# Sixteen kilobytes moved from the DMA scratch to a tile arena: two more expert-weight slots in each layer of a hybrid diffusion trunk

## The chip, the cores and the metric

The kernel runs on one core of one Trainium2 chip, in fp32 (matmul operands are fp32, or fp32r pairs of a high and a low part). The metric is the device time of one execution in microseconds; the time of a kernel is the median of its runs.

## What is computed

Two trunk layers over 256 latent tokens and 256 context tokens of width 1024. Each layer modulates and normalizes its tokens, projects them, runs four mixers (retention, window attention, neighbourhood attention, gated delta rule), merges these with sigmoid gates, projects out, and then runs a mixture of experts. Layer 0 carries all 512 tokens on; layer 1 only the 256 latent ones.

```
mod  = silu(c) @ w_mod + b_mod                       # six rows of 1024, for latent and context
h    = rmsnorm(x, norm1) * (1 + sc1) + sh1
z    = h @ w_in                                      # 1024 x 5904
ys   = retention(z), window(z), neighbourhood(z), gdn(z)
acc  = sum_i sigmoid(h @ w_merge[i]) * (ys[i] @ w_branch[i])
x    = x + g1 * (acc @ w_out)
h2   = rmsnorm(x, norm2) * (1 + sc2) + sh2
e    = top-2 experts of the best of 8 groups of 4    # 32 experts, routed by a sigmoid
x    = x + g2 * sum_e w_e * (silu(h2 @ w_e_gate[e]) * (h2 @ w_e_up[e])) @ w_e_down[e]
```

The experts' weights are 3 x 2 MB for each of the 32 experts, so each layer reads 192 loads of 1 MB.

## The kernel before

**Memory.** Nearly all tiles live in two arenas that the kernel manages itself: `arenaF` (fp32, `FKB` = 136 KB per partition, in segments `FSEG`, the last one 64 KB) and `arenaR` (fp32r, 56 KB). `Arena.alloc` takes a zone (an address range) and, unless `first` is set, the place in it that was given back longest ago. Python decides all addresses ahead of time; the framework then orders each engine's instructions by their place in the program and by estimated times, and adds the waits for tiles that are still in use. The zones are constants at the top of the file: `ZRAW` (0 to 16 KB, raw weights on their way to being split), `ZPRJ` (103 KB to the end, rings of the dense section), `ZMIX[l]` (merge, residual and expert scratch) and `ZW[l]` (the expert weights' slots). `ZW[0]` and `ZW[1]` start at 16 KB; `ZMIX[l]` starts where `ZW[l]` ends.

**The dense part of a layer** (`dense`, L1492). Projections, mixers and gates run interleaved, with weights loaded by SP into `ZRAW` (L242) and split in two by ACT and DVE or GpSimd. The gates' tanh goes to DRAM (`th`, L1356) and comes back in `merge` (L1391), where it multiplies the branch products `pbr`. The section's rings are allocated from the low end of `ZPRJ` and given back when the section ends (L1540), ahead of `merge`. By their sizes in the code they take 23 KB: five work buffers of 2 KB, `zt` 4, `prow` 3.25, `rt` 2, `jk`, `rtab` and `abw` 1 each, `ptmp` 0.5, `ab` 0.25.

**Modulation rows.** `mod` (L318) computes 2048 columns of the modulation at a time. The first call stands at the kernel's start; five more calls (40 loads of 1 MB of w_mod, 160 matmuls into `pmod`) are a filler in layer 0, of which one step is taken at a time, at places in the retention and attention part (`fill`, L346). Their zone is `ZPRJ`: a bias row `sb` of 2 KB from the low end, and for each load a buffer of 8 KB:

```python
for k in range(2):
    w = self.F.alloc((128, 4, 512), *zone)
    nc.sync.dma_start(w, wm[:, 2 * kk + k, c0:c0 + 2048].rearrange("p (j n) -> p j n", j=4))
    for j in range(4):
        nc.tensor.matmul(ps[32 * j:32 * j + 32], self.sc[:, 2 * kk + k, :], w[:, j], ...)
    self.F.free(w)
```

**Experts** (`moe`, L1898). After out-projection and routing, `wslots` (L1770) makes the slots for expert weights, 8 KB per partition (1 MB) each:

```python
slots = [(self.F, o) for o in range(ZW[l][0], ZW[l][1] - n + 1, n)]
slots.sort(key=lambda v: self.F.since(v[1], n))
...
late = 3 if l else 0
self.wq += reg[:len(reg) - late] + once + reg[len(reg) - late:]
```

`ZW` holds 9 slots in layer 0 and 11 in layer 1; layer 1 adds two of `arenaR`; and in both layers three places (two of `arenaR`, one of `ZRAW`) serve once. So 12 loads can be under way before the first matmul in layer 0, and 16 in layer 1. Slots that were given back earlier are used first. The out-projection's buffers (`ZTR`) lie on some of them, and in layer 0 the neighbourhood mixer's output `yk` lies at 95 to 103 KB until its turn, the last, in `merge`.

Experts run in pairs (`mlp`, L1822): gate (4 loads, 32 matmuls), up (4), down (4). SP issues the loads in the order gate of pair 0, up 0, gate 1, down 0, up 1, gate 2, down 1 and so on (L1800), each into the slot at the head of a queue; a slot goes back to its end after its matmuls. All loads and stores of the kernel are issued by SP, in one order.

Of the kernel before, what the change touches and what calls it, by code (L numbers as in the profile page):

```python
# [22 lines left out]
OFF = {'ret_q': 0, 'ret_k': 256, 'ret_v': 512, 'ret_g': 1024, 'win_q': 1536, 'win_k': 2048, 'win_v': 2176,  # L23
       'na_q': 2304, 'na_k': 2816, 'na_v': 3328, 'gdn_q': 3840, 'gdn_k': 4352, 'gdn_v': 4864, 'gdn_g': 5376,
       'gdn_ab': 5888}
FKB, RKB, WLO = 136, 56, 32
FSEG = (16, 16, 16, 16, 8, 64)
RSEG = (16, 16, 8, 8, 8)
KB = lambda a, b: (a * 256, b * 256)

# [4 lines left out]
      ((2, 1, 2, 1), (1, 1, 1, 1, 1, 1), (2, 1, 2, 1), (2, 2, 1, 2)))  # L35
FD = ((0, 10, 2), (6, 28, 4))
FT = 1, 3
ZW = (KB(16, 88), KB(16, 106))
ZMIX = (KB(88, FKB), KB(106, FKB))
ZYK = (KB(95, 103), KB(106, FKB))  # L40
ZATT = ((KB(16, 32), KB(72, 103)),)
ZTR = (KB(56, 88), KB(74, 98))
ZRET = (KB(48, 64), KB(72, 103)),
# [90 lines left out]
class Net:  # L134
    def __init__(self, tc, ctx, a, dbg):
# [6 lines left out]
        self.sp = p("sp", 1)  # L142
        self.F = Arena(self.big, [k * 256 for k in FSEG], F32, "arenaF")
        self.R = Arena(self.big, [k * 256 for k in RSEG], F32R, "arenaR")
# [1347 lines left out]
    def dense(self, l):  # L1492
# [25 lines left out]
        self.zone = ZATT  # L1518
        self.yk = self.F.alloc((128, 4, nt), *ZYK[l])
        self.done = {}  # L1520
# [20 lines left out]
        self.aside = False  # L1541
        self.zone = ZMIX[l]
        with self.use(1):
# [226 lines left out]
    def wslots(self, l):  # L1770
# [4 lines left out]
        self.wq = deque()  # L1775
        slots = [(self.F, o) for o in range(ZW[l][0], ZW[l][1] - n + 1, n)]
        slots.sort(key=lambda v: self.F.since(v[1], n))
# [287 lines left out]
```

## Time and profile before

| | |
|---|---|
| median of 3 runs | 2553.84 us (2551.1 to 2556.44) |
| profiled execution: its own time | 2552.03 us |
| its span, first to last instruction | 2550.3 us |
| PE busy (matmul) | 2341.4 us, 92% |
| DVE, ACT, GpSimd busy | 52%, 32%, 20% |
| bytes read from HBM, written to HBM | 609.85 MB, 30.16 MB |
| mean granted clock of TensorE | 0.970 |

The two expert stages lie at about 996 to 1470 us (layer 0) and 2085 us to the end (layer 1). Busy shares are averages over stages with different limits.

### The profile page before, as it was taken

What the parts mean: (1) busy time and instruction counts of PE and PEld (TensorE: products, weight loads), DVE (VectorE), ACT (ScalarE), POOL (GpSimd) and SP (SyncE); (2) the same over time, 40 slices, a digit from 0 to 9 for tenths busy, and PEclk for the clock granted to TensorE, in tenths of its full rate; (3) what the DMA queues carried; (4) which work ended last, traced back from release to release, by engine and by line L of the source; (5) the groups of instructions that cost most, each with busy time, mean ns of one, the idle gap of its engine ahead of it and who ended that gap; (6) DMA issues with size and microseconds to landing.
All of it is one profiled execution on the core that took longest, in us unless ns stands there. A gap on an engine that the chain in (4) does not pass through costs nothing. (4 is left out here: it accounts for less than half of the span.)

```text
span 2550.3 us, 38070 instructions
## 1 busy us (share of the span) xinstructions
PE 2341.4 (92%) x14396; PEld 1596.1 (63%) x14396; DVE 1321.4 (52%) x3284; ACT 818.2 (32%) x1810; POOL 518.0 (20%) x491
## 2 busy tenths in 40 slices
PE   6989899999999987999999989998899879999897
PEld 3777787676666884444545478998788854433332
DVE  5674754275456676333333268795777652222222
ACT  3443343244455342110101155444467321101100
POOL 2222313241210540111111221010411410000001
PEclk8999999999999998999999989999899989999999
DMA  7235425655556655999999934735236869999997
GB/s 273 83 106 159 108 84 174 201 187 205 208 186 230 222 166 191 401 420 419 420 419 419 385 91 114 210 109 149 92 102 216 266 233 420 419 420 419 420 419 315
DMA packets 269196, 642.56 MB, mean 252 GB/s; under 512 B 64336, under 2 KB 194768, under 8 KB 213072
## 3 DMA queue, kind: packets, MB, share of 16 engines
q1 hardware_dynamic: 269008, 640.07, 68.1%
q8 instruction: 115, 1.88, 0.3%
q14 instruction: 73, 0.60, 0.1%
HBM read 609.85 MB, written 30.16 MB: 251 GB/s over the span
## 5 line engine op out<-in xcount | busy, mean ns | idle before, releaser
L177 POOL TENSOR_TENSOR arenaF<-arenaF 128x512 f32<-128x512 f32 (+3 forms) x226 | 252.3, 1129 | 1217.1 <-DVE arenaF L177 933.5
L281 PE MATMUL pd<-arenaR,arenaR 128*128 128x256 f32 (+1 forms) x1152 | 359.9, 313 | 8.1 <-ACT arenaR L423 3.2
L282 PE MATMUL pd<-arenaR,arenaR 128*128 128x256 f32 (+1 forms) x1152 | 354.5, 308 | 12.4 <-DVE arenaR L177 12.1
L283 PE MATMUL pd<-arenaR,arenaR 128*128 128x256 f32 (+1 forms) x1152 | 351.9, 306 | 0.0
L177 DVE TENSOR_TENSOR arenaR<-arenaF,arenaR 128x512 fp32r<-128x512 f32 (+2 forms) x366 | 283.2, 788 | 116.6 <-ACT arenaR L249 81.8
L249 ACT ACTIVATE arenaR<-arenaF 128x512 fp32r<-128x512 f32 (+1 forms) x348 | 247.7, 721 | 207.2 <-PE pbr L282 58.6
L165 PE MATMUL pw_e_up<-arenaF,arenaF 128*64 128x512 f32 x952 | 233.6, 595 | 25.6 <-DMA arenaF<-in_w_e_up_dram 25.6
L281 PEld LDWEIGHTS pd<-arenaR,arenaR 128*128 128x128 f32 x1152 | 225.3, 196 | 27.3 <-issue 9.6
L282 PEld LDWEIGHTS pd<-arenaR,arenaR 128*128 128x128 f32 x1152 | 225.4, 196 | 23.5 <-DVE arenaR L177 15.5
L283 PEld LDWEIGHTS pd<-arenaR,arenaR 128*128 128x128 f32 x1152 | 225.3, 196 | 9.1 <-issue 2.8
L165 PE MATMUL pw_e_gate<-arenaF,arenaF 128*64 128x512 f32 x920 | 219.1, 598 | 0.0
L177 DVE TENSOR_TENSOR arenaR<-py,arenaR 128x512 fp32r<-128x512 f32 x64 | 44.3, 692 | 319.1 <-ACT arenaR L1875 318.1
L165 PE MATMUL py<-arenaF,arenaF 128*64 128x512 f32 x672 | 193.0, 594 | 3.3 <-DMA arenaF<-in_w_e_down_dram 2.4
L165 PEld LDWEIGHTS pw_e_up<-arenaF,arenaF 128*64 128x64 f32 x952 | 79.0, 137 | 164.4 <-issue 112.3
L281 PE MATMUL pgate<-arenaR,arenaR 128*128 128x512 f32 (+1 forms) x512 | 178.5, 349 | 3.0 <-ACT arenaF L688 2.1
L283 PE MATMUL pgate<-arenaR,arenaR 128*128 128x512 f32 (+1 forms) x512 | 178.1, 348 | 2.6 <-DVE arenaR L177 2.6
L282 PE MATMUL pgate<-arenaR,arenaR 128*128 128x512 f32 (+1 forms) x512 | 176.4, 345 | 0.0
L177 POOL TENSOR_TENSOR arenaR<-arenaF,arenaR 128x1024 fp32r<-128x1024 f32 (+1 forms) x48 | 111.1, 2316 | 229.3 <-ACT arenaR L249 207.3
L177 DVE TENSOR_TENSOR arenaF<-arenaF 128x128 f32<-128x128 f32 (+30 forms) x368 | 132.8, 368 | 8.0 <-ACT arenaF L864 1.8
L186 DVE SCALAR_TENSOR_TENSOR arenaF<-pw_e_up,ws,arenaF 128x512 f32<-128x512 f32 x32 | 24.0, 751 | 213.8 <-PE pw_e_up L165 213.8
L1860 ACT ACTIVATE arenaF<-pat 128x512 f32<-128x512 f32 x32 | 19.1, 597 | 360.1 <-PE pat L1858 360.1
L165 PEld LDWEIGHTS pw_e_gate<-arenaF,arenaF 128*64 128x64 f32 x920 | 63.5, 136 | 110.7 <-issue 103.2
(400 smaller groups left out, 4384.4 us busy)
## 6 DMA issues: line engine op xcount, KB each, us to landing
arenaF<-in_w_e_up_dram SPq DMA_DIRECT2D x119, 1024.0 KB, 12.1
arenaF<-in_w_e_down_dram SPq DMA_DIRECT2D x117, 1024.0 KB, 16.1
arenaF<-in_w_e_gate_dram SPq DMA_DIRECT2D x116, 1024.0 KB, 12.8
arenaF<-in_w_mod_dram SPq DMA_DIRECT2D x48, 1024.0 KB, 5.3
arenaF<-in_w_in_dram SPq DMA_DIRECT2D x92, 512.0 KB, 4.1
arenaF<-in_w_merge_dram SPq DMA_DIRECT2D x64, 512.0 KB, 4.0
arenaF<-in_w_branch_dram SPq DMA_DIRECT2D x32, 512.0 KB, 4.8
arenaF<-in_w_out_dram SPq DMA_DIRECT2D x24, 512.0 KB, 4.4
```

Of the source, the lines that this page charges most:

```text
L165: self.tc.keep_in_program_order(self.nc.tensor.matmul(out, lhs, rhs, start=start, stop=stop))
L177: (eng or self.nc.vector).tensor_tensor(out=out, in0=a, in1=b, op=op)
L186: self.nc.vector.scalar_tensor_tensor(out, a, s, b, op0=op0, op1=op1, accum_out=accum)
L249: self.nc.scalar.activation(h, src, AF.Copy)
L281: mm(ps, L[0], R[0], start=first, stop=False)
L282: mm(ps, L[0], R[1], start=False, stop=False)
L283: return mm(ps, L[1], R[0], start=False, stop=last)
L1860: nc.scalar.activation(aT[:, :, :np_], pt[:, :, :np_], AF.Copy)
```

## The change

The scratch that the program reserves in SBUF for dynamic DMAs goes from 16 KB (the default) to 2 KB per partition. `arenaF` grows by 16 KB: its last segment from 64 to 80 KB. The expert slots' zones `ZW` grow by 16 KB, so they hold 11 slots in layer 0 and 13 in layer 1. `ZMIX`, and `ZYK` in layer 1, move up by 16 KB at the same size. `ZDENSE` (16 KB to the end) and `ZPRJ` (103 KB to the end) are written with `FKB` and so grow by 16 KB.

```diff
-FKB, RKB, WLO = 136, 56, 32
-FSEG = (16, 16, 16, 16, 8, 64)
+FKB, RKB, WLO = 152, 56, 32
+FSEG = (16, 16, 16, 16, 8, 80)
...
-ZW = (KB(16, 88), KB(16, 106))
-ZMIX = (KB(88, FKB), KB(106, FKB))
-ZYK = (KB(95, 103), KB(106, FKB))
+ZW = (KB(16, 104), KB(16, 122))
+ZMIX = (KB(104, FKB), KB(122, FKB))
+ZYK = (KB(95, 103), KB(122, FKB))
...
-    nc = _bacc.Bacc("TRN2", target_bir_lowering=False, num_devices=1)
+    nc = _bacc.Bacc("TRN2", target_bir_lowering=False, num_devices=1, dynamic_dma_scratch_size=2048)
```

## Rows read from the trace of the kernel before

**Rows 1.** The page's 40 slices of the span: GB/s moved by DMA.
```profile
GB/s 273 83 106 159 108 84 174 201 187 205 208 186 230 222 166 191 401 420 419 420 419 419 385 91 114 210 109 149 92 102 216 266 233 420 419 420 419 420 419 315
```

**Rows 2.** Busy time by stretch: its length, PE, PEld, DVE, ACT, POOL, clock, DMA.
```profile
core 0: us, PE busy (x) PEld busy (x) DVE busy (x) ACT busy (x) POOL busy (x), PEclk, DMA share, GB/s
400.00:760.00 360.00, 339.61 (x2111) 243.34 (x2111) 180.50 (x500) 148.50 (x352) 93.28 (x87) 0.99 0.58 198
...
996.00:1460.00 464.00, 462.12 (x2292) 217.73 (x2290) 164.59 (x317) 47.92 (x80) 73.31 (x56) 1.00 1.00 409
...
1960.00:2060.00 100.00, 92.27 (x748) 86.58 (x746) 58.45 (x118) 45.77 (x97) 34.72 (x36) 1.00 0.78 256
...
2072.00:2080.00 8.00, 1.69 (x7) 1.51 (x7) 6.65 (x34) 0.00 (x0) 0.00 (x0) 0.50 0.63 267
2080.00:2089.00 9.00, 8.93 (x43) 5.86 (x43) 5.93 (x33) 2.03 (x5) 0.00 (x0) 0.76 0.00 0
...
2200.00:2500.00 300.00, 272.43 (x1248) 110.66 (x1248) 76.07 (x153) 29.86 (x50) 25.93 (x21) 1.00 1.01 420
```

**Rows 3.** The chain that ended last: start us, length us, what.
```profile
1977.40 5.25 DMA arenaF<-th
...
2504.18 19.89 DMA arenaF<-in_w_e_up_dram
2524.11 3.66 PE pw_e_up L165 x14
```

**Rows 4.** SP's issues in layer 1: start, duration of the group, line, how many.
```profile
1887.30 0.34 SPq L1800 DMA_DIRECT2D arenaF<-in_w_e_gate_dram  x1
...
2069.80 0.33 SPq L1800 DMA_DIRECT2D arenaF<-in_w_e_down_dram  x1
2088.76 6.50 SPq L1800 DMA_DIRECT2D arenaF<-in_w_e_up_dram  x4
...
2506.68 7.80 SPq L1800 DMA_DIRECT2D arenaF<-in_w_e_down_dram  x4
```

**Rows 5.** PE's waits, 996 to 1470 us: total, times, longest.
```profile
PE pw_e_up L165 <- DMA arenaF<-in_w_e_up_dram: 0.3, 1, 0.3
```

**Rows 6.** SP's issues in layer 0's expert stage, two rounds.
```profile
1058.37 6.77 SPq L1800 DMA_DIRECT2D arenaF<-in_w_e_down_dram  x4
...
1087.98 6.77 SPq L1800 DMA_DIRECT2D arenaF<-in_w_e_down_dram  x4
```

**Rows 7.** PE in order of time, layer 0's expert stage: an early and a late group.
```profile
1028.31 7.04 PE L165 MATMUL pw_e_up<-arenaF,arenaF 128*64 128x512 f32 x32
...
1415.85 7.52 PE L165 MATMUL pw_e_up<-arenaF,arenaF 128*64 128x512 f32 x32
```

**Rows 8.** DMA queues, whole span: packets, MB, share of 16 engines.
```profile
q1 hardware_dynamic: 269008, 640.07, 68.1%
```

**Rows 9.** SP's issues of w_mod in layer 0's attention part.
```profile
481.64 0.33 SPq L331 DMA_DIRECT2D arenaF<-in_w_mod_dram  x1
...
489.64 0.33 SPq L331 DMA_DIRECT2D arenaF<-in_w_mod_dram  x1
...
741.31 0.33 SPq L331 DMA_DIRECT2D arenaF<-in_w_mod_dram  x1
```

**Rows 10.** The page's DMA issues: count, size, median us to landing.
```profile
arenaF<-in_w_mod_dram SPq DMA_DIRECT2D x48, 1024.0 KB, 5.3
...
arenaF<-th SPq DMA_DIRECT2D x32, 256.0 KB, 3.5
```

**Rows 11.** SP's waits, 400 to 760 us.
```profile
SPq L331 <- DMA arenaF<-in_w_mod_dram: 55.5, 15, 7.0
...
SPq L331 <- PE pmod L333: 42.5, 22, 7.8
```

**Rows 12.** PE's waits, 400 to 760 us.
```profile
PE pmod L333 <- DMA arenaF<-in_w_mod_dram: 9.5, 9, 2.1
```

**Rows 13.** SP's issues in layer 0's merge.
```profile
800.32 0.69 SPq L1800 DMA_DIRECT2D arenaF<-in_w_e_gate_dram  x1
```

**Rows 14.** PE's waits, 796 to 832 us.
```profile
PE pbr L281 <- DVE arenaF L186: 3.8, 1, 3.8
```

## Prediction

> **What bounds the kernel now.** I read the slices of the page first, for the places where DMA is full: two plateaus of about 420 GB/s, the expert stages of the two layers, and before each of them a long stretch of mostly 80 to 270 GB/s [rows 1]. Then the stretches by stage, to see for each plateau whether PE is full beside DMA [rows 2]. In layer 0 (996 to 1460 us) PE is busy 462.12 of 464 us: it has no time left, so PE sets the end there. In layer 1 (2200 to 2500) PE is busy 272.43 of 300 us and the DMA share is 1.01: DMA sets the end there. The chain of waits says the same: its late part is one weight load of 19.9 us after another, up to the last matmuls [rows 3].
>
> In layer 1 a load of 1 MB costs 1.0486 MB / 420 GB/s = 2.50 us of a full DMA [rows 2]; the 19.89 us of a link of the chain are then 8 loads in flight. The plateau starts when SP gets the first slot back, at 2088.76 [rows 4]. Until then the 16 slots have taken 16 of the layer's 192 loads, from 1887.30 to 2069.80; between 2080 and 2089 DMA moves nothing at all [rows 2]. From 2088.76 on, 176 loads are left: 176 x 2.50 = 440 us, which gives 2528. The last four were issued from 2506.68 to about 2514 [rows 4], so the last landed some 20 us later, at 2534. "First free slot plus what is left" is 6 us short in 445; as a law of differences it should hold better: each load taken before 2088.76 ends the kernel 2.50 us earlier.
>
> **The change part by part.**
>
> *Two more slots in layer 1.* They cover 104 to 120 KB, where the rings of the dense section were, which are given back before the merge (its `th` loads are on the chain from 1977 [rows 3]). They are sorted ahead of the slots under the out-projection's buffers, so two loads of the second pair's gate weights go into them early, and the two slots of arenaR take the first two up loads of the second pair, which before waited for 2088.76. DMA has room for them: a share of 0.78 over 1960 to 2060, 0.63 in 2072 to 2080, nothing in the 9 us after [rows 2]. They need 5 us. Bounds: 0 if they are issued only after 2088, and -5.0 us if both land before. I take -5.0: DMA is full from there to the end, so nothing swallows it. The cover is PE's slack: 300 - 272 = 28 us in the 300 shown, far more than 5, so PE doesn't become the bound.
>
> *Two more slots in layer 0.* PE waits for a weight only once between 996 and 1460, 0.3 us [rows 5], and SP comes round every 29.61 us per pair of experts, 1058.37 to 1087.98 [rows 6], where 12 loads need 12 x 2.50 = 30.0. So DMA loses 0.4 us a pair and the stock of filled slots runs dry only at the very end: a late group of up matmuls takes 7.52 us where an early one takes 7.04 [rows 7]. Bounds: 0, and three times that stretch, 1.5 us, if the two groups of weights after it are as late. I take -1.
>
> *The scratch.* The program's transfers, 640.07 MB, went through one queue of the kind hardware_dynamic [rows 8], and every issue in the profile is SP's. The trace doesn't show the scratch. I cost it at nothing; what it would cost if loads in flight needed it stands with the rivals.
> The Trainium skill (DMA: Bandwidth & Descriptors, section SWDGE vs HWDGE vs iDMA) says that only transfers whose descriptors GpSimd writes keep rings in SBUF, and that those issued from SP never touch that path; by it this part is exactly 0. No run here shows it so far.
>
> *A side effect on layer 0's modulation loads, which the change doesn't name.* The zone ZPRJ grows from 33 to 49 KB with the arena. The dense section's rings take its first 23 KB (see above) and the bias row of `mod` 2 KB, so 8 KB were left: exactly one buffer for the 40 loads of w_mod that are strewn through the attention part. The trace has this: successive loads of w_mod are 8 us apart (481.64 and 489.64), the last goes out at 741.31 [rows 9], though one lands in 5.3 us [rows 10], and SP stands still before such an issue for 55.5 + 42.5 us [rows 11] with other loads behind it. PE pays 9.5 us in 9 waits for w_mod [rows 12]. With 16 KB more there are three buffers, so a load can go out two loads (16 us) ahead of its use, against 5.3 us of landing. In 400 to 760 PE is busy 339.61 of 360 us [rows 2], so this stage is PE's too, and its 20 us of gaps are all there is to win. Bounds: -9.5 if each of the nine waits goes and nothing takes its place; 0 if other gaps open (the order of instructions is made anew from estimates, and matmuls of `mod` that now come early no longer fill later gaps). I take the middle, -5: nine waits of about 1 us in a stream that is 94% busy should partly reappear.
>
> *What the early loads collide with.* In both layers the added loads may go out during the merge, whose `th` loads are short and urgent: the one at 1977.40 holds the chain for 5.25 us [rows 3]. In layer 0 the two new slots overlap the buffer `yk` (95 to 103 KB), so they come free in the last quarter of the merge. The like has happened before: an expert load went out at 800.32 among the merge's loads [rows 13], and PE lost 3.8 us on a branch product around there [rows 14]. Four more such loads: from 0 to 4 x 3.8 = 15 us. PE is busy 92.27 of 100 us in layer 1's merge [rows 2] with most of its early expert loads out, so most of them cost nothing visible. I take +2, half a collision.
>
> Sum: -5.0 - 1 - 5 + 2 = -9 us. Against the profiled execution's 2552.03 (span 2550.3 and 1.7 around it) that gives 2543; the median of the three runs is 1.8 above that execution, so for a median I say 2545. A measurement of this kernel tells about 0.2%, 5.1 us, from no change.
>
> **Rivals.**
>
> *Layer 1 alone.* The modulation loads pay nothing, because PE's gaps only move: -5.0 - 1 + 1.5 = -4.5, 2549. For it: 20 - 9.5 = 11 us of PE's gaps in that stage have other causes, so other work runs late there too. Against it: SP's 98 us behind w_mod. 0.24, half of it inside 0.2%.
>
> *Everything pays.* -5.0 - 1.5 - 9.5 and no collision: -16, 2538. 0.10.
>
> *The slots come too late.* SP issues in one fixed order; if the added loads are put behind an issue that waits for the routing, they reach DMA only around 2088 and the change doesn't do what it says: nothing in layer 1, and with other gaps opening at w_mod about 0 in all, 2553. Against it: SP issued nothing from 2070 to 2088 [rows 4], since it had no slot to fill. 0.08.
>
> *Slower: prefetch ahead of the `th` loads.* Place: the merges. One queue serves both; a `th` load behind two weight loads comes 2 x 2.50 = 5.0 us later than its 3.5 us [rows 10], and DVE, then PE, wait. Each collision costs 3.8 us [rows 14]. With nothing won at w_mod, two of them (7.6) eat the 6 us of the expert stages, so it decides from two on; all four give 15 - 6 = +9, 2563. 0.10.
> The Trainium skill (DMA: Bandwidth & Descriptors, section Queues, rings and completion order) says that each DMA engine takes the descriptors of one issuer's ring in order, so a late `th` can't overtake a weight load; by it a collision costs what is queued ahead. The trace agrees in one place, with the 3.8 us.
>
> *The scratch bounds the loads in flight.* One load at a time would take the 5.3 us that a load of this size takes by itself [rows 10] in place of 2.50: 384 x 2.8 = 1075 us more. Nothing in the trace speaks for it; under 0.01.
>
> **How the numbers follow.** Forecast 0.48, layer 1 alone 0.24, everything 0.10, too late 0.08, slower 0.10. Faster by over 0.2%: 0.44 of the forecast's 0.48, 0.11 of layer 1 alone, and 0.10: 0.65. Within 0.2%: 0.04 + 0.13 + 0.08 = 0.25. Slower: 0.10. The likeliest gives 2545, with its own range 2540 to 2549. The range for 8 in 10 runs from just past "everything" to 2 us past "too late": 2537 to 2555. It leaves out the slower case and a tail of the best one.
>
> **What would show it.** Right: in layer 1 eighteen expert loads issued before the first slot comes back, and 5 us less between the first gate matmul and the end; in layer 0's expert stage a length within 1.5 us of before; in the attention part w_mod loads issued in groups, PE's waits for them near 0, and the last of them well before 741. Wrong: a longer merge, with PE or DVE waiting for `th`; the same number of early loads as before; new PE gaps in the attention part of the size of those that went.

## The result, and the profile after

The changed kernel takes 2515.01 us (median of 4, 2513.18 to 2521.81) where the kernel beside it takes 2554.89: a ratio of 0.9851, 95% interval 0.9831 to 0.9871. It is faster by about 40 us, more than four times the 9 us of the forecast and outside its range. Timed twice more, each time beside the kernel before on the same chip, it gave 0.9848 and 0.9835.

The page of the kernel after: busy times, and the DMA's slices, which answer to [rows 1].

```profile
PE 2312.6 (92%) x14396; PEld 1586.1 (63%) x14396; DVE 1333.0 (53%) x3284; ACT 815.6 (32%) x1810; POOL 519.2 (21%) x491
...
GB/s 283 112 108 162 110 85 170 221 201 265 206 154 246 222 141 248 400 419 419 420 419 419 324 105 132 199 109 145 93 119 223 269 250 419 420 419 419 420 419 320
```

PE is busy 92% of the span, as before, but 28.8 us less: the same 14396 records take less time. (A record is one row of the trace; an fp32 product of `py` or `pmod` leaves two.) So most of the gain lies in what the profile calls busy, not in PE's waits. To find where, here are the windows of both kernels by the same four stages: layer 0's attention part from the first filler product to the first branch product, layer 0's merge, layer 0's expert stage and layer 1's. Before:

```profile
411.50:784.50 373.00, 354.24 (x2189) 252.42 (x2189) 197.60 (x557) 165.17 (x397) 96.60 (x94) 0.99 0.59 201
...
784.50:908.10 123.60, 117.11 (x576) 93.08 (x575) 78.97 (x147) 47.10 (x96) 40.44 (x28) 0.97 0.68 223
995.80:1476.30 480.50, 474.05 (x2337) 225.07 (x2336) 177.09 (x334) 50.99 (x85) 81.03 (x64) 1.00 0.97 397
2085.20:2550.30 465.10, 424.69 (x1968) 172.00 (x1968) 121.50 (x258) 48.89 (x82) 38.60 (x30) 0.99 0.97 400
```

After:

```profile
409.30:763.00 353.70, 335.34 (x2188) 252.59 (x2188) 206.09 (x564) 164.41 (x400) 97.78 (x94) 0.98 0.62 211
...
763.00:879.80 116.80, 114.79 (x575) 90.48 (x574) 78.91 (x140) 45.88 (x94) 41.04 (x28) 1.00 0.72 241
969.50:1446.20 476.70, 469.74 (x2337) 218.62 (x2336) 176.83 (x333) 51.30 (x86) 81.35 (x65) 1.00 0.96 396
2052.40:2511.40 459.00, 422.85 (x1969) 173.37 (x1968) 121.83 (x260) 49.04 (x82) 38.53 (x30) 1.00 0.97 401
```

The attention part is 19.3 us shorter, the merge 6.8, the expert stages 3.8 and 6.1: 36.0 of the span's 38.9 us. The other stretches differ by 6 us at most, in both directions. The expert stages and the merge repeat well: over all the profiles layer 1's expert stage takes 458.9 to 460.8 us with the two new slots and 463.8 to 465.2 without, and layer 0's merge 123.2 to 125.2 us where its zone stays and 116.7 to 118.8 where it moves (but for the two runs further down whose new order shifts that boundary). In the attention part PE does the same products in 18.9 us less of busy time; its idle time is about the same (18.8 and 18.4 us), and its clock is not higher.

SP's issues after, which answer to [rows 9] and [rows 4] (start, duration of the group, line, how many):

```profile
434.54 2.41 SPq L331 DMA_DIRECT2D arenaF<-in_w_mod_dram  x2
459.93 2.42 SPq L331 DMA_DIRECT2D arenaF<-in_w_mod_dram  x2
490.79 0.88 SPq L331 DMA_DIRECT2D arenaF<-in_w_mod_dram  x2
...
650.48 0.33 SPq L331 DMA_DIRECT2D arenaF<-in_w_mod_dram  x1
...
1855.69 0.34 SPq L1800 DMA_DIRECT2D arenaF<-in_w_e_gate_dram  x1
...
2037.15 0.33 SPq L1800 DMA_DIRECT2D arenaF<-in_w_e_down_dram  x1
2056.11 0.80 SPq L1800 DMA_DIRECT2D arenaF<-in_w_e_up_dram  x2
```

The loads of w_mod now go out in groups of up to three, the last 91 us earlier than in [rows 9]. From 1855.69 to 2037.15 there are 18 expert loads before the first slot comes back at 2056.11; in [rows 4] there were 16. PE's waits after, 400 to 740 us, which answer to [rows 12], and behind them a wait of before (400 to 760 us) that [rows 12] doesn't show:

```profile
PE ppt L1330 <- DVE arenaF L186: 7.2, 3, 3.7
PE ppt L1330 <- DVE arenaF L177: 3.4, 1, 3.4
...
PE pmod L333 <- issue: 0.8, 1, 0.8
```

```profile
PE ppt L1330 <- DVE arenaF L186: 2.5, 2, 2.2
```

No wait for a w_mod load is left, but the transposes `ppt` now wait 10.6 us for the softmax on DVE, where they waited 2.7 before.

### The profile page after: what moved, and what is told of

Same layout as the page of the kernel before. It is cut to its first block, busy times and chain, and to the rows that moved or that the text cites. A ratio compares the mean times of both kernels' runs of the same rounds, so it can differ in the third digit from the quotient of the medians.

```text
span 2511.4 us, 38022 instructions
## 1 busy us (share of the span) xinstructions
PE 2312.6 (92%) x14396; PEld 1586.1 (63%) x14396; DVE 1333.0 (53%) x3284; ACT 815.6 (32%) x1810; POOL 519.2 (21%) x491
## 5 line engine op out<-in xcount | busy, mean ns | idle before, releaser
L165 PE MATMUL pw_e_up<-arenaF,arenaF 128*64 128x512 f32 x952 | 225.2, 594 | 20.0 <-DMA arenaF<-in_w_e_up_dram 20.0
L165 PE MATMUL py<-arenaF,arenaF 128*64 128x512 f32 x608 | 176.0, 593 | 2.8 <-DMA arenaF<-in_w_e_down_dram 1.9
L165 PEld LDWEIGHTS pw_e_up<-arenaF,arenaF 128*64 128x64 f32 x952 | 71.8, 137 | 160.0 <-issue 123.1
```

The costliest lines, as they stand in the source:

```text
L165: self.tc.keep_in_program_order(self.nc.tensor.matmul(out, lhs, rhs, start=start, stop=stop))
```

## The parts of the change, each by itself

**The scratch.** This is the kernel before, with `dynamic_dma_scratch_size=2048` and nothing else.

> Before with the scratch of 2 KB alone; no zone changes. Both theories: within 0.2% of before (5 us), the same order of instructions on every engine. If the scratch itself or the shift of addresses that it brings were worth something, it would show here.

Measured: 0.9996 (0.9978 to 1.0013). The smaller scratch costs and brings nothing that can be told from 0.2%. That fits what the Trainium skill (DMA: Bandwidth & Descriptors, section SWDGE vs HWDGE vs iDMA) says of transfers that SP issues.

**The modulation loads.** Slots and zones as before; only the filler's zone gets the new 16 KB. In the second run it gets 8 of them.

```diff
-ZDENSE, ZIN, ZPRJ, ZRAW = KB(16, FKB), KB(16, 48), KB(103, FKB), KB(0, 16)
+ZDENSE, ZIN, ZPRJ, ZRAW = KB(16, 136), KB(16, 48), KB(103, 136), KB(0, 16)
...
-            self.filler = itertools.chain(*(self.mod(*q) for q in ((0, 1, ZPRJ), ...
+            self.filler = itertools.chain(*(self.mod(*q) for q in ((0, 1, KB(103, 152)), ...   # second run: 144
```

> Only the filler's zone for w_mod grows (three buffers instead of one); expert slots, the merge's zones and everything else stay where they were before. Theory 'order': with the modulation loads no longer late, PE's order around them is made with fewer changes between kinds of matmul, and the same matmuls run closer together; so the stretch from the first filler load to the first branch product falls from 370.7 to about 352 us, PE's busy time in it from 352 to about 333, and the kernel by 19 to 27 us (19 of that stretch, up to 7 of the merge behind it, whose first yr buffer waits for the last w_mod). Rival 'waits only': what was lost were PE's nine waits of 9.5 us; the kernel falls by at most 10 and PE's busy time stays at 352. Rival 'slots and room': the gain hangs on the slots and the larger merge zone; within 4 us of before.

> As the run with three buffers, but the filler's zone is 8 KB larger instead of 16: two buffers for w_mod. A load can then go out one load, about 8 us, ahead of its use, against 5.3 us of landing. Theory 'order': it comes on time, so nearly the whole gain of three buffers, 15 to 25 us. Rival 'the gain grows with the distance': half of what three buffers give, about 10 us. Rival 'slots and room': within 4 us of before.

Measured: 0.9916 (0.9892 to 0.9940) with three buffers, 21.8 us by the medians; 0.9928 (0.9905 to 0.9951) with two, 17.4 us. So this side effect is over half of the whole gain, and two buffers can't be told from three. The attention part with three buffers, to be read against the 373.00 of before:

```profile
413.30:768.60 355.30, 336.30 (x2189) 252.31 (x2188) 204.59 (x563) 163.24 (x397) 97.80 (x94) 0.98 0.61 206
```

It is 17.7 us shorter, with 17.9 less of PE busy time: nearly what the whole change does there. Merge and expert stages stay within 1 us of before, so the gain in the merge that was expected of this run didn't come.

**Slots and merge.** The first run is the change with the filler held to 33 KB; the second has only the slots, put into the new 16 KB; the third moves only layer 0's merge zone.

```diff
+((0, 1, KB(103, 136)), ...                           # all three: one buffer for w_mod
...
+        slots += [(self.F, o * 256) for o in (136, 144)]      # slots only; ZW, ZMIX as before
...
-ZMIX = (KB(88, 136), KB(106, 136))
+ZMIX = (KB(104, FKB), KB(106, 136))                           # room only; ZW as before
```

> The change as it is, but the filler keeps its 33 KB, so one buffer for w_mod as before. Theory 'order': the stretch from the first filler load to the first branch product stays at 371 us (within 3) with PE busy 352 in it; what is left is the merge and the expert stages, 10 to 17 us in all, of which layer 1's expert stage 5 to 6. Rival 'slots and room': 30 to 40 us, as the whole change.

> Only two more expert slots in each layer, in the new 16 KB (136 to 152 KB); one buffer for w_mod and the merge's zones as before. Theory: layer 1's expert stage 5 us shorter (two loads more before the first slot comes back), layer 0's 4 to 5 us (its up matmuls stay at 6.97 us a group instead of stretching to 8.3 from the ninth group on), merge of layer 0 within 2 us of before; 8 to 11 us in all. Rival 'a hidden cost of prefetch in the merge': less than 6.

> Only layer 0's merge zone moves, from 88-136 KB (of which 8 KB are taken by yk until its last quarter) to 104-152 KB (48 KB free at once); slots and w_mod's one buffer as before. Theory 'room': the stretch from the first branch product to the first router product falls from 123.6 to about 118 us, nothing else moves: 4 to 7 us. Rival 'the merge gains through the slots' or 'through the earlier end of w_mod': within 2 us of before.

Measured: together 0.9942 (0.9924 to 0.9961), 15.2 us; slots alone 0.9963 (0.9951 to 0.9976), 9.6 us; room alone 0.9992 (0.9980 to 1.0005), 3 us by the medians, which can't be told from no change, though its merge is shorter. The product of three buffers and of slots with merge is 0.9916 x 0.9942 = 0.9858, the whole change 0.9851: the parts add up.

Slots alone: layer 1's expert stage goes from 465.10 to 460.00 us and layer 0's from 485.30 to 480.80, each here up to the next norm's first transpose, which is some 5 us later than in the windows above. The merge, with the early loads beside it, takes 124.40 and layer 1's 110.5 (123.60 and 110.3 before), so these loads cost at most 1 us there. First layer 0's stage before, then both stages of the slots-only run:

```profile
995.80:1481.10 485.30, 474.07 (x2338) 225.09 (x2337) 180.10 (x345) 53.88 (x92) 82.28 (x66) 1.00 0.96 395
```

```profile
1005.70:1486.50 480.80, 469.86 (x2337) 219.37 (x2336) 179.97 (x345) 53.86 (x92) 82.20 (x66) 0.99 0.97 399
2091.80:2551.80 460.00, 422.90 (x1969) 172.71 (x1968) 121.46 (x258) 48.96 (x82) 38.55 (x30) 1.00 0.97 400
```

Room alone: the merge's window, and PE's waits there, 760 to 912 us:

```profile
796.30:914.40 118.10, 116.30 (x574) 92.06 (x573) 78.74 (x147) 46.52 (x95) 40.66 (x28) 0.99 0.70 226
```

```profile
PE pbw L1436 <- DVE bwc L1433: 0.9, 1, 0.9
PE pout L281 <- ACT arenaR L1407: 0.9, 1, 0.9
```

The merge is 5.5 us shorter and the 3.8 us wait of [rows 14] is gone, though the early expert loads still go out beside it. What ended that wait is in SP's rows. Before, the first pair of `th` loads is issued 21 us after the merge's start at 784.50, and SP waits ahead of it for the attention product `py`, 4.8 us at the longest; a `th` load can depend on `py` only through the place that it goes to. In the room-only run the pair goes out 4 us after the merge's start at 796.30. First two rows of before (SP's waits, 784 to 832 us, and its issues), then the issue in the room-only run:

```profile
SPq L1391 <- PE py L1337: 5.2, 2, 4.8
...
805.82 1.19 SPq L1391 DMA_DIRECT2D arenaF<-th  x2
```

```profile
800.15 0.81 SPq L1391 DMA_DIRECT2D arenaF<-th  x2
```

So the wait was not the queue behind an expert load: the merge had no place for `th`. Its zone of before begins at 88 KB, among the addresses up to 103 KB that attention and `yk` use. In the run with slots and merge this wait is gone too, and by the medians that run gains 5.6 us more than the slots alone (on two chips). That the room-only kernel shows less in its time is not explained: the profiled execution, the slowest of its 12, had an attention part of 382.1 us, and the same part, in the order of before and with one buffer, took 373.0, 371.8, 374.1 and 379.0 us in the profiles of before, of the small scratch, of slots with merge and of slots alone. It differs by 10 us from one profile to the next, so a difference of a few us there means little in a single profile.

## Why the attention part got shorter: order or lateness

With three buffers PE's order changes between the 2057th and the 4041st of the 11494 matmul instructions that can be pinned as shown below, and nowhere else. Two things therefore came together: loads that are on time, and a new order. An order can be pinned without any wait, by edges between neighbours that hold only for issue (shortened here):

```python
pe = [i for i in nc.cur_bb.bb.instructions if i.engine == mybir.EngineType.PE and ...]
for a, b in zip(order, order[1:]):
    tc.add_manual_dep(pe[b], pe[a].name, mybir.DependencyInfo(mybir.DependencyClass.NoSync, ...), reason="pin")
```

One run has three buffers with the order of before, the other one buffer with the order that three buffers give.

> The kernel with three buffers for w_mod, but all PE matmuls pinned (issue order only, no added waits) to exactly the order that they have in the kernel before; so the loads can come early and PE's order is the old one. Theory 'order and lateness both': with gaps sorted by the pair of matmul kinds on either side, the three-buffer run lost 10.6 of its 17.7 us by a different mix of neighbours and 7.2 by shorter waits; so here the stretch from the first filler load to the first branch product falls by about 7 (to 366), and the kernel by 7 to 10 us. Rival 'order alone': within 3 us of before. Rival 'lateness alone': the whole 18 us of the stretch, 22 of the kernel, whatever the order.

> The kernel before with its one buffer for w_mod, but all PE matmuls pinned to exactly the order that they have in the kernel with three buffers. Rival 'order alone': the whole gain, 15 to 22 us. Theory 'order and lateness both': this order runs the matmuls of two loads back to back, and with one buffer the second load can only be issued when the first one's matmuls are over; each of the 20 pairs then makes PE wait for a load that takes 5.3 us or more, so 60 to 130 us slower than before.

Measured: early loads in the old order 0.9966 (0.9952 to 0.9980), 9.3 us; and once more:

> Three buffers with PE's old order once more, on the chip of the other three: 0.9966 of before, within 0.002, by every theory; what the old order with products rejoined is compared with.

0.9952 (0.9934 to 0.9971), 13.4 us. The new order with late loads: 1.0494 (1.0469 to 1.0520), 126 us slower; PE then waits for w_mod:

```profile
PE pmod L333 <- DMA arenaF<-in_w_mod_dram: 112.3, 23, 7.8
```

So early loads by themselves are worth 9 to 13 us, about the 9.5 that [rows 12] gave as a bound; the new order adds the other 8 to 13 of the 21.8 (a difference of runs on different chips), and it pays only with the buffers. The attention part of the two old-order runs:

```profile
413.00:776.20 363.20, 353.80 (x2188) 251.35 (x2188) 197.71 (x557) 165.28 (x397) 96.61 (x94) 0.99 0.62 200
```

```profile
408.40:773.30 364.90, 355.44 (x2190) 252.69 (x2189) 198.20 (x558) 165.14 (x397) 96.66 (x94) 0.98 0.59 199
```

Against the 373.00 of before, early loads in the old order leave PE's busy time where it was (354 us) and halve its idle time, 18.8 to 9.4 us: that is the waits for w_mod. The new order then takes 18 us off the busy time and gives 10 us of idle time back (336 of 355 us). So a PE that was 97% busy ran an order in which the same products cost more.

**What in the order?** Call products that write the same tile one kind. Counted from the trace's records of this part, neighbours are of different kinds 332 times in the old order and 256 times in the new, and 297 and 326 records start within 0.01 us of the one before. The first suspect was the change of kind. Two runs pin the changed kernel's order with runs of projection and gate products put together.

> The changed kernel with PE's order pinned to its own, but for the attention part of layer 0, where each run of at most six projection or gate matmuls that is followed by at most 16 others is put behind these, to the next run of its kind: 232 runs of one kind in place of 284. Theory 'changes of kind cost PE time': early loads with the new order had 76 changes fewer than early loads with the old order and the stretch was 7.9 us shorter, about 0.10 us a change (an estimate from those two runs); 52 fewer are worth about 5 us, so 5 us less than the changed kernel run beside it and PE's busy time in the stretch 5 us lower. Rival 'the mix of neighbours is worth nothing by itself': within 2 us of the changed kernel, busy time the same. Rival 'delay costs more': the matmuls put off are waited for, 3 us or more slower than the changed kernel.

> As the run with longer runs in the attention part, and also in the delta-rule part before it (runs of at most three, put behind at most twelve others: 294 runs in place of 339). Theory: 45 changes fewer there, about 4.5 us more, so some 9 to 10 us less than the changed kernel. Rival: PE waits there for DVE and ACT anyway, and what is put off is late: 0, or a loss of some us in the first 411 us.

Measured: 0.9863 (0.9842 to 0.9883) and 0.9878 (0.9859 to 0.9897), beside the changed kernel:

> The changed kernel again, beside the others on the same chip. Every theory: 0.985 of the kernel before, within 0.002; it is what the two kernels with longer runs are compared with.

0.9848 (0.9824 to 0.9873). So neither is faster, and the second is more likely slower (2525.5 against 2519.5 us): the theory fails as stated. The part's own window can't be compared, since its end has moved in the new order. From the first filler product to the first router product the first of these runs took 477.1 us with PE busy 450.6, the changed kernel 472.3 with 451.9: busy time fell by 1 us where 5 were expected, and idle time rose by 6. PE gets new waits, of the transposes for ACT, which empties their PSUM tile:

```profile
PE ppt L1330 <- ACT arenaF L1331: 3.9, 5, 2.0
```

The changed kernel has no such row. That the products put off had been covering this is likely but not shown. Fewer changes alone don't pay.

The second suspect was products that lie in different halves of the array (`py` writes 64 of 128 PSUM partitions with each) and start side by side when they are neighbours. One run rejoins 29 such groups in the old order, one parts those of `py` in the changed kernel's order with the kinds left as they are, by the order of its loops:

```diff
-        for j in range(nj):
-            for e in range(2):
+        for e in range(2):
+            for j in range(nj):
```

> Three buffers and PE's old order, as in the run with early loads and old order, but 29 groups of products that the old order parts are put side by side again (12 pairs of py, 15 of psc, 2 groups of pmod); changes of kind 346 instead of 356, so nearly as many. Theory 'parted products': counted over four kernels, the stretch without its waits moves by 0.30 to 0.37 us for each pair of records that start together, so these 29 give back 6 to 9 us of the 7.9 that the old order costs: near the run with three buffers, 0.993 or less of before. Rival 'changes of kind': ten fewer, 1 us; as the old order. Rival 'neither': within 2 us of the old order.

> The changed kernel with the same sequence of kinds on PE, but inside each py tile the four products of one column half come first and then those of the other, so that no two neighbours lie in different halves. Theory 'parted products': 16 records of py, which took 1.88 us, take about 16 x 0.21 = 3.4; for the 320 records of the kernel 20 to 30 us slower than the changed kernel, 12 to 18 of them in the stretch. Rivals: changes of kind are the same, so within 2 us of the changed kernel.

Measured: parted 0.9892 (0.9869 to 0.9915), 8 to 13 us slower by the medians than the changed kernel (2527.5 against 2519.5 and 2514.7, timed apart from it), where 20 to 30 were expected. The rows of a `py` group of 16 and of one of 8 (start, duration), first in the changed kernel timed again, then parted:

```profile
579.39 1.95 PE L1337 MATMUL py<-arenaF,arenaF 128*64 128x256 f32 x16
...
613.14 1.08 PE L1337 MATMUL py<-arenaF,arenaF 128*64 128x256 f32 x8
```

```profile
579.02 2.86 PE L1337 MATMUL py<-arenaF,arenaF 128*64 128x256 f32 x16
...
614.57 1.09 PE L1337 MATMUL py<-arenaF,arenaF 128*64 128x256 f32 x8
```

Parting costs 0.91 us in a group of 16; six of them in this part make 5.5 us, and the part was 5.7 longer (360.2 against 354.5). The mechanism is real but weaker than expected: a group of 16 takes 2.86 us parted and not 3.4, and a group of 8 loses nothing, since its products still start in pairs 0.01 us apart. Rejoined in the old order: 0.9948 (0.9930 to 0.9966), no different from the old order's 0.9952. Its attention part:

```profile
413.00:775.30 362.30, 348.98 (x2189) 248.01 (x2189) 198.03 (x565) 164.61 (x397) 97.05 (x94) 0.99 0.60 202
```

PE is busy 4.8 and 6.5 us less than in the two runs of the old order, but the part is only 0.9 and 2.6 us shorter: the rest went into idle time. Only 16 more pairs of records came to start together, none of them of `py`, so this run tests half of what it set out to. It shows at most 2.6 of the 8 to 10 us that the order is worth in this part as the price of parted products. The remainder has no single cause that a run here showed; cheaper products and newly opened waits came together in every order that was tried.

**The same cure without memory, and a better order.** One run has half-size loads in the 8 KB of the kernel before; two rejoin in the changed kernel the products that its own order parts.

> The kernel before, with no memory moved, but each load of w_mod split into two of half the size (two of the four column blocks each), so that the 8 KB of one buffer hold two. Theory 'lateness and order': the next half can come while the last one is multiplied; the stretch falls by a part of what two full buffers gave (16 of 18 us), 4 to 10 us, if the four column blocks still run side by side. Rival 'blocks apart': the four 32-column products of one load no longer start together, and each load costs up to 0.5 us more, 20 us in 40 loads: slower than before by 5 to 20 us.

> The changed kernel with the 11 groups rejoined that its own order still parts in that stretch (3 pairs of py, 4 of psc, 4 groups of pmod). Theory 'parted products': 2 to 4 us less than the changed kernel (0.9848 to 0.9851 of before), so about 0.9837. Rivals: no difference.

> The changed kernel with the 11 parted groups of layer 0 rejoined, and the 3 of layer 1 too. Theory 'parted products': the run that parted 58 pairs of records on purpose lost 5.6 us in the stretch, 0.1 us a pair, and the rejoined run's stretch was 3.0 us shorter than the changed kernel's, so 2 to 4 us less than the changed kernel beside it. Rival: no difference, within 2 us.

> The changed kernel on the same chip, 0.985 of before; what the rejoined one is compared with.

Measured: half loads 1.0094 (1.0073 to 1.0115), slower by 24 us. The rival "blocks apart" held, and cost more than its 5 to 20 us: four records of `pmod` took 1.05 us, as long as eight in the changed kernel. First the half loads, then the changed kernel:

```profile
424.41 1.05 PE L334 MATMUL pmod<-arenaF,c_sc 128*32 128x512 f32 x4
```

```profile
433.43 1.07 PE L333 MATMUL pmod<-arenaF,c_sc 128*32 128x512 f32 x8
```

Rejoined: 0.9836 (0.9812 to 0.9860), and in both layers 0.9823 (0.9798 to 0.9848) beside the changed kernel's 0.9835 (0.9813 to 0.9856). The attention part was 3.0 us shorter in each, 351.5 and 351.2 against 354.5 and 354.2, but only 4 and 5 more pairs of records start together, and whole kernels of 2513.34 and 2514.67 us can't be told apart. So whether rejoining pays here is not shown.

## Why the prediction was wrong, step by step

- **Layer 1's slots, -5.0: right.** There are 18 loads before the first slot is back, and the stage is 5.1 us shorter in the slots-only run. Nothing swallowed it.
- **The scratch, 0: right.** The run with the small scratch alone gave 0.9996.
- **Layer 0's slots, -1, bounded at -1.5: too small.** The step took the late group of [rows 7] as a matter of the end of the stage. It is not: from the ninth of sixteen on, every group of up products takes longer, 7.19 to 8.39 us. Before, the tenth group, and after, the one in its place:

```profile
1264.82 7.76 PE L165 MATMUL pw_e_up<-arenaF,arenaF 128*64 128x512 f32 x32
```

```profile
1238.70 7.04 PE L165 MATMUL pw_e_up<-arenaF,arenaF 128*64 128x512 f32 x32
```

  Summed over the groups of before, the excess over 7.04 is 4.3 us, and the stage lost 4.5 in the slots-only run. The single wait of 0.3 us in [rows 5] was no measure: the profile counts a product that comes late within its group as busy.
- **The modulation loads, -5, bounded at -9.5: the step that failed.** It named the mechanism, the one buffer, and then took PE's idle time as all that could be won ("its 20 us of gaps are all there is to win"). Measured were 21.8 us. In the old order the bound was right, and the guess of half of it too low: early loads took 9.4 us off PE's idle time and 9 to 13 off the kernel. But the order is made anew, which stood there only as a risk, and the new order cut what the step held fixed, PE's busy time, by 18 us. That was worth as much again as the waits.
- **Collisions with the `th` loads, +2: the wrong sign.** The price was read from [rows 14], a wait that had another cause, the merge's place for `th`; so the 3.8 us are no sign that a `th` load queues behind a weight load, and what the prediction reads into them ("The trace agrees in one place") doesn't hold. The slots alone made the two merges less than 1 us longer. The change moved `ZMIX[0]` off the addresses that attention and `yk` use, which the prediction didn't price, and the merge lost 5.5 us in the room-only profile.
- **The rivals.** "Everything pays" was the nearest, at 23 us from the result. The two that bet on nothing at w_mod, and the slower one, are ruled out by the runs above.
- **Left open:** why the rest of the new order is cheaper, and why the room alone shows only 3 us. Part by part the runs give 5.1, 4.5, 21.8 and 5.5 us, 37 of the 40. Layer 1 in front of its expert stage has no part in the gain: from the end of layer 0's expert stage to layer 1's first branch product the profile has 493.7 us before and 492.5 after, and 490.2 and 492.4 in the changed kernel's two other profiles.

## What to carry to other kernels

A size written into many zones changes every one of them: before pricing the part that the change names, list all users of the constant and ask which of them has exactly one buffer. PE's idle time bounds what an earlier load can bring only as long as the order stays; expect an order that is made from estimates to change with the buffers. Compare the duration of equal groups early and late in a stage, since busy time can hide lateness. To tell order from lateness, pin the one order onto the other's buffers, both ways.

## What the runs showed of the hardware

Two products in different column halves of the array start 0.01 us apart when they are neighbours in PE's order: 16 records take 1.95 us. When the loops put all of one half first, they take 2.86 us; 8 records take 1.08 and 1.09. In the parted group of 16 the records start 0.21 to 0.27 us apart up to 579.93, and from 579.94 on a second row of starts runs beside the first; records of one half are never that close. So the second half starts while three records of the first, which stand ahead of it, have yet to start, and in the group of 8 likewise. The Trainium skill (TensorE: Matmul & The Clock Gate, section Part 3: Packing small matmuls — row/col tiling) says that products in different column groups run at once, and that starts and ends keep the program's order. The rows agree with the first; with the second the starts of the parted groups don't agree, and parting costs less than it would by that.
